# Differential attention: one projection of q and k for a head pair, with a weight ring of raw 2, hi 3, lo 3

## The chip, the core and the metric

The kernel runs on one core of a Trainium2 chip. The engines of that core are TensorE (PE in the profile, with its weight loads as PEld), VectorE (DVE), ScalarE (ACT) and GpSimd (POOL); SyncE (SP) issues most transfers. The metric is the device time of one execution in microseconds (us).

## The reference, cut to what matters

Two transformer blocks run over 512 tokens of 1024 features, in float32: a pooling mixer and a latent attention (MLA), each with a SwiGLU feed-forward stage, then a final norm, differential attention and a mixture of 16 experts. The change lies in the differential attention:

```python
def diff_attention(x, w_in, q_gain, k_gain, lq1, lk1, lq2, lk2, subln, w_out, lambda_init):
    H, dh = DA_HEADS, DA_HEAD_DIM
    q, k, v = jnp.split(x @ w_in, [2 * H * dh, 4 * H * dh], axis=-1)
    q = rmsnorm(q.reshape(B, T, H, 2, dh), q_gain) * (dh ** -0.5)
    k = rmsnorm(k.reshape(B, T, H, 2, dh), k_gain)
    v = v.reshape(B, T, H, 2 * dh)
    ...
    for s in range(0, T, QBLOCK):
        ...
        p = jax.nn.softmax(sc, axis=-1)
        pd = p[:, :, 0] - lam * p[:, :, 1]
        outs.append(jnp.einsum('bhqk,bkhe->bqhe', pd.astype(v.dtype), v[:, :e]))
    o = rmsnorm(jnp.concatenate(outs, axis=1), subln) * (1.0 - lambda_init)
    return o.reshape(B, T, H * 2 * dh) @ w_out
```

## The kernel before

**Products.** Each float32 factor is held as a high and a low part, so that one product is three matmuls (high by high, low by high, high by low), added up in an accumulator. Activations are kept transposed: `xh[k]`, `xl[k]` hold 128 features of all 512 tokens, for the eight slices k of the 1024 features. PSUM has eight banks of 512 float32 columns here: four of tag `acc`, two of tag `t` (transposes), two of tag `s` (scores).

**Weights.** `Stream` (`self.ws`) brings the weights as items of up to 2048 columns. `load` has SP transfer an item into a `raw` buffer; `split_part` makes a quarter's high part on ACT (`hi<-raw`) and its low part on DVE or POOL (`lo<-raw,hi`); `pump` does one such quarter if the rings `BUFS` (line 47) have room; `take` hands an item to its consumer and first splits what is missing; `release` gives `hi` and `lo` back. The expert weights use the same buffers later.

**Order.** All engines work in program order. The program's order is made when the kernel is built: generators are tasks of `Sched`, which runs the ready task of lowest rank by the times that `Plan` estimates for each engine. `get` takes a free PSUM bank, waiting in this planned time, and `put` gives it back. So a change in one place can move instructions of the rest of the stage on every engine.

**Differential attention.** `attention` runs two tasks. `feed` projects the four head pairs one after the other by `da_project(p, out)`; pair 0 and 1 at once, pair 2 and 3 when enough blocks of the earlier pairs are over (`LEAD`). `blocks` (higher priority) runs eight heads with four query blocks each: `da_scores` (tiles `pss`, `p`), `da_values` (`acc<-v,pth`, `on`, `o`). When all pairs are projected the heads' outputs are split (`oh`, `ol`) and the output products (`acc<-oh,hi` and so on) begin.

**A pair's projection.** In `da_project` the tokens are the stationary factor and the weights stream: for s = q, k, v and for each of four token tiles j, eight slices k with three matmuls of 256 columns, two tiles to an `acc` bank. Each of q, k and v is an item of 2048 columns. In pair 0 the first seven slices of two tiles of q come first (`early`), because the last slice `xh[7]` is the last that the feed-forward stage delivers. After the last slice of the first tile `da_norm` is started: it sums squares over the features (`pst<-ones,ss`), takes roots on POOL (`r1`, `r2`), and yields `r12` per token and R, r1 spread over all partitions by `pst<-ident,r`; then it updates `x` slice by slice on DVE. Each finished bank of q or k goes to `part(s, jj, ps)`: wait for `r12`, square on ACT (`sq<-acc`), sum by groups of 64 on DVE (`st<-sq`), scale (`st`, `rqkv`), power on POOL (`rqk<-rqkv,mhalf`), scale (`rqk`), and `qn<-acc,rqk` on DVE, which frees the bank. When both banks of q (or of k) are through, `turned(s)` transposes them head by head (`pst<-ident,qn`), and `q_parts` and `k_parts` split the result on ACT and DVE (`qh`, `ql`, `kh`, `kl`, `klh`, `kll`). `v_part` scales and splits v.

The lines that the steps touch are 47 (rings), 1340 to 1346 (`r12`), 1355 to 1489 (`da_project`), and the layout of `da_in` in `_host`.

## Time and profile before

| | us |
|---|---|
| three runs: median (lowest to highest) | 1568.91 (1567.87 to 1570.69) |
| the profiled execution | 1568.89 |
| its span on the core | 1567.1 |
| PE busy | 1495.6 (95%) |
| PE weight loads busy | 1233.7 (79%) |
| DVE busy | 1017.4 (65%) |
| ACT busy | 782.9 (50%) |
| POOL busy | 508.8 (32%) |

The stages by the order of time on PE: pooling to 36 us, feed-forward to about 430, MLA to 660 with its output products, feed-forward to 939, differential attention to about 1214 with its output products, routing to 1237, experts to the end. A busy share is an average over these stages. Matmuls are pipelined: a matmul's recorded duration overlaps the next one's, so the distance between two starts tells what one costs. In a row of the trace in order of time the brackets at the end give the idle time ahead of it on its engine and what ended that; the names are those of the program, output first.

### The profile page before, as it was taken

How to read it: one execution, taken by the hardware profiler on the slowest of the kernel's cores; microseconds unless marked ns; L12 is line 12 of the kernel's file. 1: busy time of each engine (PE TensorE's matmuls, PEld its weight loads, DVE VectorE, ACT ScalarE, POOL GpSimd, SP SyncE). 2: the span in 40 equal slices, each digit the busy share in tenths (PEclk: the TensorE clock that was granted, in tenths of full speed). 3: DMA queues.
4: the chain of work that ended last, by engine and by line, in shares of the span. 5: the costliest groups of instructions: out<-in, count | busy, mean ns of one | idle time of the engine just before them, and what ended most of it. 6: DMA issues, size and time to landing. Idle time of an engine off the chain costs nothing. (4 is left out here: it accounts for less than half of the span.)

```text
span 1567.1 us, 21562 instructions
## 1 busy us (share of the span) xinstructions
PE 1495.6 (95%) x7752; PEld 1233.7 (79%) x7752; DVE 1017.4 (65%) x1668; ACT 782.9 (50%) x1585; POOL 508.8 (32%) x382
## 2 busy tenths in 40 slices
PE   8999999999999999999999999999989699999996
PEld 7788888888878888888888889998978466666664
DVE  6564344445477754443444466988984699999996
ACT  5323222323366633332233345787783478787884
POOL 4322122311231113321232223322222466565553
PEclk9999999999999999999999999999989699999998
DMA  6121333223210223214322232211068889999961
GB/s 241 61 107 56 116 111 108 73 75 119 69 63 28 68 108 121 99 42 142 108 86 86 74 119 84 78 55 68 28 202 296 261 302 362 345 355 360 348 206 27
DMA packets 69935, 221.61 MB, mean 141 GB/s; under 512 B 7616, under 2 KB 16960, under 8 KB 56640
## 3 DMA queue, kind: packets, MB, share of 16 engines
q1 hardware_dynamic: 56448, 201.03, 35.9%
q0 software_dynamic: 4064, 14.16, 3.7%
q10 hardware_dynamic: 9312, 5.01, 1.1%
q8 instruction: 62, 1.02, 0.3%
q14 instruction: 49, 0.40, 0.1%
HBM read 208.63 MB, written 11.53 MB: 140 GB/s over the span
## 5 line engine op out<-in xcount | busy, mean ns | idle before, releaser
L341 POOL TENSOR_TENSOR lo<-raw,hi 128x512 fp32r<-128x512 f32 (+1 forms) x157 | 224.4, 1439 | 694.4 <-ACT hi L341 592.4
L341 PE MATMUL acc<-xh,hi 128*128 128x512 f32 x744 | 290.5, 390 | 0.3 <-ACT xh L341 0.3
L341 PE MATMUL acc<-xl,hi 128*128 128x512 f32 x744 | 289.6, 389 | 0.3 <-DVE xl L341 0.3
L341 PE MATMUL acc<-xh,lo 128*128 128x512 f32 x744 | 289.5, 389 | 0.0
L341 DVE TENSOR_TENSOR wl<-raw,wh 128x512 fp32r<-128x512 f32 x288 | 268.1, 982 | 6.1 <-ACT wh L341 5.7
L341 ACT ACTIVATE hi<-raw 128x512 fp32r<-128x512 f32 (+1 forms) x378 | 208.8, 607 | 86.1 <-issue 59.8
L341 DVE TENSOR_TENSOR lo<-raw,hi 128x512 fp32r<-128x512 f32 (+1 forms) x221 | 215.9, 987 | 19.6 <-ACT hi L341 18.9
L341 ACT ACTIVATE wh<-raw 128x512 fp32r<-128x512 f32 x384 | 211.8, 621 | 15.8 <-PE acc L341 10.0
L341 POOL TENSOR_TENSOR wl<-raw,wh 128x512 fp32r<-128x512 f32 x96 | 147.1, 1533 | 119.4 <-ACT wh L341 90.8
L341 PEld LDWEIGHTS acc<-xh,hi 128*128 128x128 f32 x744 | 139.7, 188 | 29.6 <-ACT xh L341 0.7
L341 PEld LDWEIGHTS acc<-xl,hi 128*128 128x128 f32 x744 | 139.7, 188 | 29.1 <-DVE xl L341 0.6
L341 PEld LDWEIGHTS acc<-xh,lo 128*128 128x128 f32 x744 | 139.6, 188 | 29.1
L341 DVE TENSOR_TENSOR u<-acc,R 128x512 f32<-128x512 f32 x44 | 30.4, 691 | 181.0 <-PE acc L341 181.0
L341 PE MATMUL acc<-hh,hi 128*128 128x512 f32 x352 | 136.9, 389 | 0.0
L341 PE MATMUL acc<-hl,hi 128*128 128x512 f32 x352 | 136.9, 389 | 0.0
L341 PE MATMUL acc<-hh,lo 128*128 128x512 f32 x352 | 136.9, 389 | 0.0
L341 ACT ACTIVATE hh<-t 128x512 fp32r<-128x512 f32 x44 | 27.8, 632 | 218.4 <-DVE t L341 218.4
L341 DVE TENSOR_TENSOR x<-acc,x 128x512 f32<-128x512 f32 x59 | 40.5, 690 | 121.0 <-PE acc L341 120.9
L341 PE MATMUL acc<-hi,xh 128*128 128x256 f32 x384 | 111.0, 289 | 0.0
L341 PE MATMUL acc<-lo,xh 128*128 128x256 f32 x384 | 108.7, 283 | 0.6 <-DVE lo L341 0.6
L341 PE MATMUL acc<-hi,xl 128*128 128x256 f32 x384 | 108.5, 283 | 0.0
L341 PE MATMUL acc<-wl,teh 128*96 128x512 f32 x256 | 102.5, 401 | 3.3 <-POOL wl L341 1.7
(314 smaller groups left out, 2917.9 us busy)
## 6 DMA issues: line engine op xcount, KB each, us to landing
raw<-moe_w SPq DMA_DIRECT2D x200, 256.0 KB, 7.1
raw<-moe_w SPq DMA_DIRECT2D x46, 1024.0 KB, 7.3
raw<-ffn_gu SPq DMA_DIRECT2D x43, 1024.0 KB, 4.8
raw<-ffn_dn SPq DMA_DIRECT2D x32, 704.0 KB, 4.0
raw<-da_in SPq DMA_DIRECT2D x12, 1024.0 KB, 4.7
raw<-mla_up SPq DMA_DIRECT2D x4, 832.0 KB, 4.4
raw<-mla_o_a SPq DMA_DIRECT2D x12, 256.0 KB, 4.3
raw<-da_o_a SPq DMA_DIRECT2D x12, 256.0 KB, 3.9
```

Of the source, the lines that this page charges most:

```text
L341: r = f(*args, **kw)
```

## The change

- q and k of a pair are projected together. `da_in` is laid out anew on the host: a pair's first two items hold q's and k's 256 columns side by side, slices 0 to 3 in the first and 4 to 7 in the second; the third item is v's, as before. For each token tile the eight slices now take three matmuls of 512 columns each, which fill one `acc` bank. Two items are held during this phase. v keeps its 256 columns and two tiles to a bank.
- In pair 0 the first seven slices of all four tiles come first, then the last slices.
- `part(j, ps)` handles one tile with q and k side by side. Its scaling uses `r12qk`, a small table that `da_norm` fills with two more copies.
- `turned` for q and for k start when all four tiles are through; v's projection follows the tiles at once.
- `pump` is called twice per tile in both phases.
- The rings are raw 2, hi 3, lo 3 instead of raw 3, hi 3, lo 2, for the whole kernel.

```diff
--- before.py
+++ after.py
@@ -44,7 +44,7 @@
 GATHER = 7.0
 CAP = 96
 SLACK = -1.0
-BUFS = {"raw": 3, "hi": 3, "lo": 2}
+BUFS = {"raw": 2, "hi": 3, "lo": 3}
 EPS = 1e-6
 WINDOWS = (2, 4, 8, 16)
 LAMBDA_INIT = 0.8 - 0.6
@@ -1344,6 +1344,10 @@
         self.r12q = c.tile([P, NT], F32, name="r12q")
         nc.vector.tensor_scalar(self.r12q, r12, 0.125, None, op0=OP.mult)
         self.r12 = r12
+        self.r12qk = c.tile([P, NT, 8], F32, name="r12qk")
+        for i, r in enumerate((self.r12q, r12)):
+            nc.vector.tensor_copy(self.r12qk[:, :, 4 * i:4 * i + 4],
+                                  r[:, :, None].to_broadcast([P, NT, 4]))
         R = self.bcast(r1, "R1", ps[0])
         self.put("t", 2)
         for d in range(KT):
@@ -1356,7 +1360,8 @@
         nc, sched = self.nc, self.sched
         qn = {}
 
-        def part(s, jj, ps):
+        def part(j, ps):
+
             yield from self.wait("r12")
             q = self.tmp("sq")
             nc.scalar.activation(q, ps, AF.Square)
@@ -1364,31 +1369,27 @@
             st = self.small.tile([P, 8], F32, name="st", tag="st", bufs=6)
             nc.vector.tensor_reduce(st, q.rearrange("p (a b) -> p a b", b=64), axis=AX.X,
                                     op=OP.add)
-            sh = [P, 2, 4]
-            v = st.rearrange("p (a b) -> p a b", b=4)
-            j = slice(2 * jj, 2 * jj + 2)
-            nc.vector.tensor_tensor(v, v, self.r12s[:, j][:, :, None].to_broadcast(sh), op=OP.mult)
+            nc.vector.tensor_scalar(st, st, self.r12s[:, j:j + 1], None, op0=OP.mult)
             r = self.rstd(st, 64, "rqk")
             yield r
-            f = r.rearrange("p (a b) -> p a b", b=4)
-            rr = (self.r12q if s == 0 else self.r12)[:, j]
-            nc.vector.tensor_tensor(f, f, rr[:, :, None].to_broadcast(sh), op=OP.mult)
+            nc.vector.tensor_tensor(r, r, self.r12qk[:, j], op=OP.mult)
             t = self.tmp("qn")
             nc.vector.tensor_tensor(t.rearrange("p (a b) -> p a b", b=64),
                                     ps.rearrange("p (a b) -> p a b", b=64),
                                     r[:, :, None].to_broadcast([P, 8, 64]), op=OP.mult)
             self.put("acc")
             yield t
-            qn[s, jj] = t
-            if (s, 1 - jj) in qn:
-                sched.spawn(turned(s), 1)
+            qn[j] = t
+            if len(qn) == NT:
+                for s in range(2):
+                    sched.spawn(turned(s), 1)
 
         def turned(s):
             for hd in range(2):
                 pt = yield from self.get("t")
                 for j in range(NT):
-                    c = (j % 2) * 256 + hd * P
-                    self.turn(pt[:, j * P:(j + 1) * P], qn[s, j // 2][:, c:c + P])
+                    c = s * 256 + hd * P
+                    self.turn(pt[:, j * P:(j + 1) * P], qn[j][:, c:c + P])
                 yield pt
                 out["qk"[s] + str(hd)] = yield from (q_parts(pt) if s == 0 else k_parts(pt))
 
@@ -1452,41 +1453,48 @@
 
         xh, xl = self.xh, self.xl
 
-        def product(w, ps, j, ks):
-            o = ps[:, (j % 2) * 256:(j % 2 + 1) * 256]
+        def product(ws, o, j, ks, n):
             t = slice(j * P, (j + 1) * P)
+            per = KT // len(ws)
             for k in ks:
-                c = slice(k * 256, (k + 1) * 256)
+                w, c = ws[k // per], slice(k % per * n, (k % per + 1) * n)
                 self.mm(o, xh[k][:, t], w[0][:, c], start=(k == 0), stop=False)
                 self.mm(o, xl[k][:, t], w[0][:, c], start=False, stop=False)
                 self.mm(o, xh[k][:, t], w[1][:, c], start=False, stop=(k == KT - 1))
-                if k == 3:
+                if k % 4 == 3:
                     self.ws.pump()
-                if k % 4 == 3 and k < KT - 1:
+                    if k < KT - 1:
+                        yield 0.0
+
+        w = [self.ws.take(), self.ws.take()]
+        ps = [None] * NT
+        if p == 0:
+
+            for j in range(NT):
+                ps[j] = yield from self.get("acc")
+                yield from product(w, ps[j], j, range(KT - 1), T)
+        for j in range(NT):
+            if ps[j] is None:
+                ps[j] = yield from self.get("acc")
+            yield from product(w, ps[j], j, range(KT - 1 if p == 0 else 0, KT), T)
+            if p == 0 and j == 0:
+                sched.spawn(self.da_norm(), 0)
+            if j == NT - 1:
+                for x in w:
+                    self.ws.release(x)
+            sched.spawn(part(j, ps[j]), 1, ps[j])
+            yield 0.0
+        w = [self.ws.take()]
+        for jj in range(2):
+            ps = yield from self.get("acc")
+            for j in range(2):
+                yield from product(w, ps[:, j * 256:(j + 1) * 256], 2 * jj + j, range(KT), 256)
+                if j == 0:
                     yield 0.0
-
-        for s in range(3):
-            w = self.ws.take()
-            ps = [None, None]
-            early = (p, s) == (0, 0)
-            if early:
-
-                for jj in range(2):
-                    ps[jj] = yield from self.get("acc")
-                    yield from product(w, ps[jj], 2 * jj, range(KT - 1))
-            for j in range(NT):
-                if ps[j // 2] is None:
-                    ps[j // 2] = yield from self.get("acc")
-                begun = early and j % 2 == 0
-                yield from product(w, ps[j // 2], j, range(KT - 1 if begun else 0, KT))
-                if early and j == 0:
-                    sched.spawn(self.da_norm(), 0)
-                if j == NT - 1:
-                    self.ws.release()
-                if j % 2:
-                    i = j // 2
-                    sched.spawn(part(s, i, ps[i]) if s < 2 else v_part(i, ps[i]), 1, ps[i])
-                yield 0.0
+            if jj == 1:
+                self.ws.release(w[0])
+            sched.spawn(v_part(jj, ps), 1, ps)
+            yield 0.0
 
     def da_scores(self, d, hd, qb, h, done):
         nc = self.nc
@@ -2118,8 +2126,10 @@
         w = w[0].reshape(KT, P, 4, 2, P)
         o[name + "_a"] = f(w[:6].transpose(2, 1, 3, 0, 4).reshape(4, P, 1536))
         o[name + "_b"] = f(w[6:].transpose(1, 2, 3, 0, 4).reshape(P, 2048))
-    o["da_in"] = f(inp["da_w_in_2"][0].reshape(KT, P, 3, 4, 256).transpose(3, 2, 1, 0, 4)
-                   .reshape(4, 3, P, 2048))
+    w = inp["da_w_in_2"][0].reshape(KT, P, 3, 4, 256)
+    qk = w[:, :, :2].reshape(2, 4, P, 2, 4, 256).transpose(4, 0, 2, 1, 3, 5).reshape(4, 2, P, 2048)
+    v = w[:, :, 2].transpose(2, 1, 0, 3).reshape(4, 1, P, 2048)
+    o["da_in"] = f(np.concatenate([qk, v], axis=1))
     we = np.concatenate([inp["moe_w_group_2"][0], inp["moe_w_router_2"][0]], axis=1)
     o["router"] = f(we.reshape(KT, P, 20).transpose(1, 0, 2))
     o["router_b"] = f(np.concatenate([inp["moe_b_group_2"][0], inp["moe_b_router_2"][0]]))
```

**Where instructions move.** PE, first head pair: three last rows of the projection before the transposes `pst<-ident,r` of `da_norm`, and what stands behind them (`acc<-hi,xh` is a projection matmul, xh stationary and hi the weights; waits in brackets are for an engine's earlier instructions). Before:

```order
L341 MATMUL acc<-hi,xh 128x256
L341 MATMUL acc<-hi,xl 128x256
L341 MATMUL acc<-lo,xh 128x256
L341 MATMUL pst<-ident,r_7119 128x128 [waits Pool_49]
L341 MATMUL pst<-ident,r_7119 128x128 x3
L341 MATMUL acc<-hi,xh 128x256
L341 MATMUL acc<-hi,xl 128x256
L341 MATMUL acc<-lo,xh 128x256
```

Now:

```order
L341 MATMUL acc<-hi,xh 128x512
L341 MATMUL acc<-hi,xl 128x512
L341 MATMUL acc<-lo,xh 128x512
L341 MATMUL pst<-ident,r_7176 128x128 [waits Pool_49]
L341 MATMUL pst<-ident,r_7176 128x128 x3
L341 MATMUL acc<-hi,xh 128x256 [waits DVE_49,Activation_49]
L341 MATMUL acc<-hi,xl 128x256
L341 MATMUL acc<-lo,xh 128x256
```

The transposes stood in the middle of q's second tile, with q and k to go; they now stand between the last matmuls of q and k and the first of v, which takes a bank that DVE and ACT have to free.

DVE, first head pair: from a reduction of a part's squares (`st<-sq`) to the first `qn` (`lo` is a weight's low part, `x` the update by `da_norm`). Before, from the first part's reduction:

```order
L341 TENSOR_REDUCE st<-sq 128x8 [waits Activation_49]
L341 TENSOR_TENSOR st<-st,r12s 128x8 [waits DVE_49]
L341 TENSOR_SCALAR rqkv<-st 128x8 [waits DVE_49]
L341 TENSOR_TENSOR lo<-raw,hi 128x512 [waits Activation_49]
L341 SCALAR_TENSOR_TENSOR x<-x,vecs,R_7164 128x512
L341 TENSOR_REDUCE st<-sq 128x8 [waits Activation_49]
L341 TENSOR_TENSOR st<-st,r12s 128x8 [waits DVE_49]
L341 TENSOR_SCALAR rqkv<-st 128x8 [waits DVE_49]
L341 TENSOR_TENSOR rqk<-rqk,r12q 128x8 [waits Pool_49]
L341 TENSOR_TENSOR qn<-acc,rqk 128x512 [waits DVE_49,PE_49]
```

Now, from the third part's reduction (the first and second part's three rows each stand right ahead):

```order
L341 TENSOR_REDUCE st<-sq 128x8 [waits Activation_49]
L341 TENSOR_SCALAR st<-st,r12s 128x8 [waits DVE_49]
L341 TENSOR_SCALAR rqkv<-st 128x8 [waits DVE_49]
L341 TENSOR_REDUCE st<-sq 128x8 [waits Activation_49]
L341 TENSOR_SCALAR st<-st,r12s 128x8 [waits DVE_49]
L341 TENSOR_SCALAR rqkv<-st 128x8 [waits DVE_49]
L341 SCALAR_TENSOR_TENSOR x<-x,vecs,R_7211 128x512
L341 TENSOR_TENSOR rqk<-rqk,r12qk 128x8 [waits Pool_49]
L341 TENSOR_TENSOR qn<-acc,rqk 128x512 [waits DVE_49]
```

The first `qn` stood behind the reductions of two parts; it now stands behind those of four.

ACT, last head pair: around the last two instructions of `v_part` (`v<-acc`). Before:

```order
L341 ACTIVATE kh<-kh 64x512 [waits Activation_49]
L341 ACTIVATE kl<-kl 64x512 [waits Activation_49]
L341 ACTIVATE v<-acc,r_7154 128x2x128 [waits PE_49]
L341 ACTIVATE v<-acc,r_7154 128x2x128
L341 ACTIVATE klh<-klh 64x512 [waits DVE_49]
L341 ACTIVATE kll<-kll 64x512 [waits DVE_49]
L341 ACTIVATE pth<-pst 128x512 [waits PE_49]
```

Now:

```order
L341 ACTIVATE v<-acc,r_7198 128x2x128 [waits PE_49]
L341 ACTIVATE v<-acc,r_7198 128x2x128
L341 ACTIVATE qh<-pst,vecs 64x512 [waits PE_49]
L341 ACTIVATE ql<-pst,vecs 64x512
L341 ACTIVATE kh<-pst,vecs 64x512 [waits PE_49]
L341 ACTIVATE kl<-pst,vecs 64x512
L341 ACTIVATE kh<-kh 64x512 [waits Activation_49]
L341 ACTIVATE kl<-kl 64x512 [waits Activation_49]
L341 ACTIVATE o<-pst,sub 128x256 [waits PE_49]
L341 ACTIVATE klh<-klh 64x512 [waits DVE_49,Pool_49]
L341 ACTIVATE kll<-kll 64x512 [waits DVE_49]
```

k of that pair's first head was split ahead of the last v, but for the two copies `klh` and `kll`; now it is split behind it, and q of the second head (`qh`, `ql`) stands in between.

## Rows read from the trace of the kernel before

**Rows 1.** The page, part 1: busy time, share of the span and instructions.

```profile
PE 1495.6 (95%) x7752; PEld 1233.7 (79%) x7752; DVE 1017.4 (65%) x1668; ACT 782.9 (50%) x1585; POOL 508.8 (32%) x382
```

**Rows 2.** Busy time by stage (stretch, length, engines, PEclk, DMA share, GB/s).

```profile
440.00:660.00 220.00, 216.35 (x1146) 182.01 (x1145) 140.48 (x259) 110.66 (x242) 54.71 (x53) 1.00 0.21 72
1000.00:1120.00 120.00, 116.85 (x955) 115.08 (x954) 106.90 (x292) 90.04 (x230) 35.07 (x28) 1.00 0.15 54
```

**Rows 3.** Groups by line and form, PE, 930 to 1140 us (count | busy us, mean ns | idle before).

```profile
L341 PE MATMUL acc<-lo,xh 128*128 128x256 f32 x384 | 108.7, 283 | 0.6 <-DVE lo L341 0.6
```

**Rows 4.** PE in time, last matmuls of the feed-forward stage (start, duration, us).

```profile
935.64 0.39 PE L341 MATMUL acc<-hh,lo 128*128 128x512 f32 x1
...
939.27 0.28 PE L341 MATMUL acc<-hi,xh 128*128 128x256 f32 x1
```

**Rows 5.** PE in time, first pair: row sums, transposes, projection.

```profile
944.66 1.84 PE L341 MATMUL pst<-ones,ss 128*128 128x1 f32 x16
946.37 0.36 PE L341 MATMUL acc<-hi,xh 128*128 128x256 f32 x1
...
949.32 1.05 PE L341 MATMUL pst<-ident,r 128*128 128x128 f32 x8
...
950.45 0.28 PE L341 MATMUL acc<-lo,xh 128*128 128x256 f32 x1
...
959.08 0.28 PE L341 MATMUL acc<-lo,xh 128*128 128x256 f32 x1
```

**Rows 6.** DVE in time, first pair: reductions, scale, qn, x.

```profile
951.53 0.69 DVE L341 TENSOR_REDUCE st<-sq 128x8 f32<-128x512 f32 x1 [1.78 <-ACT sq L341]
...
952.53 0.68 DVE L341 TENSOR_TENSOR lo<-raw,hi 128x512 fp32r<-128x512 f32 x1
...
955.28 0.16 DVE L341 TENSOR_TENSOR rqk<-rqk,r12q 128x8 f32<-128x8 f32 x1
955.54 0.69 DVE L341 TENSOR_TENSOR qn<-acc,rqk 128x512 f32<-128x512 f32 x1
...
959.01 0.74 DVE L341 SCALAR_TENSOR_TENSOR x<-x,vecs,R 128x512 f32<-128x512 f32 x1
```

**Rows 7.** ACT in time, first pair: R and first square.

```profile
950.41 0.60 ACT L341 ACTIVATE R<-pst 128x512 f32<-128x512 f32 x1 [6.79 <-PE pst L341]
950.90 0.59 ACT L341 ACTIVATE sq<-acc 128x512 f32<-128x512 f32 x1
```

**Rows 8.** POOL in time, first pair: first power.

```profile
945.89 1.03 POOL L341 TENSOR_TENSOR r<-r1v,mhalf 128x4 f32<-128x4 f32 x1 [1.23 <-DVE r1v L341]
```

**Rows 9.** PE in time, the attention's end.

```profile
1127.74 0.60 PE L341 MATMUL pst<-ident,p 128*128 128x128 f32 x4
...
1130.99 0.34 PE L341 MATMUL pss<-kll,ql 128*128 128x128 f32 x1 [0.21 <-ACT kll L341]
...
1133.54 0.41 PE L341 MATMUL acc<-v,pth 128*128 128x256 f32 x1
...
1136.31 0.41 PE L341 MATMUL acc<-v,ptl 128*128 128x256 f32 x1
```

**Rows 10.** Busy time by stretch at the attention's end.

```profile
1131.00:1138.00 7.00, 6.13 (x27) 5.98 (x28) 3.71 (x15) 3.89 (x13) 0.00 (x0) 0.51 0.00 0
1138.00:1144.80 6.80, 3.19 (x15) 1.80 (x14) 6.31 (x20) 6.58 (x18) 0.70 (x1) 1.00 0.32 86
```

**Rows 11.** The transfers of da_in.

```profile
DMA to landing us min/median/max: 4.7/4.7/5.5
```

**Rows 12.** PE in time, first output product.

```profile
1151.25 0.78 PE L341 MATMUL acc<-oh,hi 128*128 128x512 f32 x1
```

**Rows 13.** ACT in time, last head pair's splits.

```profile
1124.93 0.67 ACT L341 ACTIVATE kh<-pst,vecs 64x512 fp32r<-64x512 f32 x1
...
1127.50 0.63 ACT L341 ACTIVATE kh<-kh 64x512 fp32r<-64x512 f32 x1
...
1128.79 0.84 ACT L341 ACTIVATE v<-acc,r 128x256 fp32r<-128x256 f32 x2
```


## The prediction

> **What bounds the kernel now.** I read the page first: TensorE (PE) is busy 95% of the span, the next engine, VectorE (DVE), 65% [rows 1]. Then the busy time by stage: from 1000 to 1120 us, where differential attention projects q, k and v of the later head pairs between the score blocks of the earlier ones, PE is idle for 3.2 us of 120 at its upper clock (1.00, which is 2.4 GHz), and DVE is busy 89% [rows 2]. So a microsecond less on PE there is nearly a microsecond less of the whole, a pause of PE is lost, and DVE is close behind. After 1120 us no projection is left to fill the waits of the attention, and the clock falls to its lower level (0.51, 1.2 GHz) for a stretch [rows 10]. Last come the views in order of time of PE, DVE, ScalarE (ACT) and GpSimd (POOL) around the first pair's projection, since the change rewrites it.
>
> **The change, part by part.**
>
> *Fewer, longer matmuls.* The projections are 1152 matmuls of 256 columns, in three groups of 384 of which one is shown [rows 3]; 768 of them are q and k and become 384 of 512 columns. Recorded durations overlap, so the price is the distance between starts. In the 512-column stream of the stage before it is (939.27 - 935.64) / 16 = 0.2269 us [rows 4]; in the 256-column stream it is (959.08 - 950.45) / 72 = 0.1199 us [rows 5]. Hence 768 x 0.1199 = 92.1 us become 384 x 0.2269 = 87.1 us: **-5.0 us**, 1.25 in each pair. Bounds: -5.0, and 0 if a long one costs as much here as two short ones.
>
> The Trainium skill, "TensorE: Matmul & The Clock Gate", section "Back-to-back issue gap", gives columns / 2.4 + 2.5 ns for a lone gap at the full clock. By that page this would be, as an estimate, 2.5 ns for each two, 1.0 us in all, and the sum below would end 4 us higher; the rows show 13 ns for each two, and the rows decide.
>
> *The accumulators of the first pair.* This step decides, I think. There are four accumulator banks ("acc"). Before, the first pair's q takes two, its k the other two, and v gets the first one back only after k. After, each of the four token tiles of q and k takes a bank, all four are opened with seven of eight slices before any last slice, and v follows at once. A bank comes back when `part` has written its `qn`; `part` first needs the norms of `da_norm`, and that starts when the first tile's last slice is done. The two PE pieces in the section on the change show it: before, short matmuls without a wait stand behind the transposes `ident,r`; after, v's first matmul stands there and waits for DVE and ACT.
>
> Count from the start of the sums `ones,ss`. PE has 1.71 us of sums (944.66 to 946.37), then only nine matmuls (9 x 0.2269 = 2.04 us) and 1.05 us of `ident,r`: it runs dry at +4.8 us [rows 5]. The chain that frees the first bank: POOL's first power is done at 946.92, +2.26 [rows 8], so `ident,r` starts when PE reaches it, +3.75; its copy R on ACT begins 1.09 us later (949.32 to 950.41), +4.84; the first square 0.49 us after that, +5.33 [rows 5, 7]; the first reduction 0.63 us later, +5.96 [rows 6]. From here the order on DVE tells: all four parts' reductions stand ahead of the first `qn`, each 1.00 us with its two small steps (951.53 to 952.53), so +9.96; then the 0.74 us update of x, 0.26 us for the scale (955.28 to 955.54) and 0.69 us for `qn`: +11.65 us [rows 6]. POOL's power for eight columns, about twice the 1.03 us for four [rows 8], hides behind the reductions. Before, the chain took 944.66 to 956.23, 11.6 us as well, covered by 99 projection matmuls. PE now stands still for 11.65 - 4.8: **+6.9 us**. Bounds: 6 and 8, since the nearest rows leave only single steps of up to 1.0 us (a reduction, a split between) in doubt.
>
> The Trainium skill, "Perfetto Trace Analysis", section "Matmuls", says that independent matmul groups should rotate through the PSUM banks, so that one's evacuation overlaps the next group's matmuls, and that larger matmuls are more efficient. The two pull apart here: in this pair the rows give the second 1.25 us and the first 6.9 us.
>
> *The clock after that pause.* Near 1131 us the pauses of the attention's end (one of 0.21 us is shown, its neighbours are 0.5 to 0.9) go over into 7 us at the lower level [rows 9, 10], where short matmuls start every (1136.31 - 1133.54) / 13 = 0.213 us [rows 9] instead of 0.120. A pause of 7 us should bring such a stretch. What falls into the pause costs nothing; if half of it, 3.5 us, falls on v's matmuls, 44% of that is lost: **+1.5 us**, bounds 0 (no fall) and 3.1 (all 7 us on work).
>
> *Pairs 1 to 3.* Here the banks' evacuation is covered by score blocks. But q and k now end together, their transposes and splits bunch, and DVE, at 89%, keeps its work while PE's shrinks by 3.75 us: I take a quarter of that as eaten by new waits, **+1.0 us**, bounds 0 and 3.75.
>
> *The ring.* A 1 MB transfer lands in 4.7 us, 5.5 at most [rows 11], and a gate-and-up tile feeds 48 long matmuls, 48 x 0.2269 = 10.9 us, so two raw buffers hide the load. q and k are held together while v is split, and each phase of a pair has eight chances to split, as many as q and k have quarters. The one wait for a split weight in the projections, 0.6 us [rows 3], may go. Zero; bounds -0.6 and, if the cover is gone once, +1. PE's order also differs in the last third of the earlier (MLA) attention, whose stage idles 3.65 of 220 us [rows 2]: zero, bounds -1.5 and +1.5. The scaling on DVE keeps its count, 16 parts of 128x512: zero.
>
> *The end of the attention.* From the last projection (1127.74) to the first output product (1151.25) it takes 23.5 us [rows 9, 12]. Afterwards, by the ACT pieces in the section on the change, ACT splits the first head's k, and the second head's q ahead of that, behind the last v instead of ahead of it: two v (0.84 together), four splits (0.67 each), four copies (0.63 each) [rows 13], 6.0 us until the first score block can end, where before it ended 3.6 us after the last projection (1130.99 + 0.34 [rows 9]). Against these 2.4 us, 20 value matmuls and 14 transposes have left this stretch, some 3 us. I take zero; -10 and +5 belong to the rivals.
>
> *Sum.* The profiled execution took 1568.89 us (span 1567.1); the median of the three runs is 1568.91, the same. -5.0 + 6.9 + 1.5 + 1.0 = +4.4: **1573.3 us**.
>
> **The rivals.**
>
> *The end of the attention shrinks (the other side).* Place: between the last projection and the first output product. In 1138 to 1144.8 us PE was busy 3.19 of 6.8 us [rows 10]. If the work that has left takes such a gap with it, 6.8 us go, and with fewer pauses the clock stays up for the rest, some 3 us more: -10, 1563.3 us. It decides once more than 4.4 us are won there. For it: fewer items, output products one score block earlier. Against: the longer queue on ACT.
>
> *The pause is milder.* The clock stays up and no new waits come: -5.0 + 6.9 = +1.9, 1570.8 us. For it: when v runs, ACT and DVE have just emptied their queues. Against: the shorter pauses near 1131 us already went with the lower clock.
>
> *The bunched splits delay the later pairs.* If the first score block of the last pair starts 2.4 us late as above, with nothing gained behind it, and the two pairs before lose half of that each, +5 in all: 1578.3 us. For it: DVE at 89%.
>
> *The long matmuls do not save here*, so that the change does not do what it says: +5.0, 1578.3 us too. Against: the stage right before shows 0.2269 us.
>
> **How the numbers follow.** Forecast 1573.3, own range 1571.3 to 1575.5: 0.40. Milder pause 1570.8: 0.25. Bunched splits 1578.3: 0.20. No saving: 0.05. Shorter end 1563.3: 0.10. A measurement of this kernel can tell about 0.2%, 3.1 us, from no change, so 1565.8 to 1572.0 counts as the same. Slower: 0.31 of the forecast's 0.40 and the two high cases, 0.56. The same: 0.09 of the forecast, the milder pause and a tenth of the shorter end, 0.35. Faster: 0.09. The range leaves out most of the shorter end below and the upper third of the two high cases: 1566.0 to 1580.0.
>
> **What would show it.** In the profile after: one pause of PE of 6 to 8 us ahead of v's first matmul, ended by DVE's `qn`; a lower granted clock right behind it; 384 matmuls of 512 columns in the projections, 0.227 us apart; the chain from `ones,ss` to the first `qn` again 11.6 us long. The forecast is wrong if that pause is under 4 us, if the stretch from the last projection to the first output product changes by more than 5 us, or if PE waits for split weights or raw transfers in any stage.

## The result

In four executions each, the changed kernel took 1592.5 us (median; 1589.6 to 1600.6) and the kernel before 1569.8 us (1567.9 to 1571.7). The ratio is **1.0153 (95% interval 1.0112 to 1.0194)**: slower, as forecast, but by 22.7 us where 4.4 were forecast, and above the upper end of the range (1580). The profiled execution of the changed kernel took 1594.4 us with a span of 1592.6, 25.5 more than the 1567.1 of before.

Part 1 of its page, to be held against [rows 1], shows 384 matmuls less and PE busy *longer*:

```profile
PE 1501.8 (94%) x7368; PEld 1220.7 (77%) x7368; DVE 1016.3 (64%) x1669; ACT 782.7 (49%) x1585; POOL 516.2 (32%) x383
```

A lower clock makes each matmul take longer, so busy time alone does not tell where the 25.5 us went. The places where PE starts something new do. The table gives the starts of five PE rows in each trace (first projection matmul, first matmul of the second pair, last projection matmul, first and last output product) and the distances between them.

| us | before | after | difference | forecast |
|---|---|---|---|---|
| start of the first projection | 939.3 | 945.6 | +6.4 | 0 |
| first pair | 38.5 | 46.9 | +8.4 | +7.15 (6.9 + 1.5 - 1.25) |
| pairs 1 to 3, to the last projection matmul | 149.8 | 160.0 | +10.2 | -2.75 (1.0 - 3.75) |
| from there to the first output product | 23.6 | 20.1 | -3.5 | 0 |
| output products, first to last | 62.5 | 65.7 | +3.2 | 0 |
| from the last output product to the end of the span | 353.4 | 354.2 | +0.8 | 0 |
| sum | 1567.1 | 1592.6 | +25.5 | +4.4 |

So the first pair went as forecast, and two stages that I had put at zero and below cost 16.6 us. The busy time by stage of the changed kernel (columns as in [rows 2], whose two stretches come first; then pairs 1 to 3 and the output products, and below them the same two stages of the kernel before):

```profile
440.00:660.00 220.00, 214.07 (x1118) 179.31 (x1118) 140.69 (x254) 107.15 (x235) 54.18 (x50) 0.98 0.19 63
1000.00:1120.00 120.00, 109.30 (x656) 97.42 (x655) 101.01 (x284) 89.57 (x226) 28.32 (x23) 0.94 0.17 60
...
992.56:1152.55 159.99, 149.29 (x915) 133.81 (x914) 132.97 (x368) 114.62 (x291) 41.69 (x33) 0.96 0.18 62
...
1172.69:1238.35 65.66, 63.99 (x342) 54.07 (x343) 39.90 (x90) 30.28 (x78) 15.16 (x14) 0.97 0.72 247
```

```profile
977.78:1127.62 149.84, 145.78 (x1189) 143.18 (x1187) 132.93 (x364) 115.13 (x290) 41.37 (x32) 1.00 0.17 61
1151.25:1213.69 62.44, 62.14 (x333) 53.19 (x332) 40.46 (x79) 30.00 (x73) 18.09 (x16) 0.97 0.87 295
```

In 1000 to 1120 us PE was idle for 3.2 us before and is for 10.7 now, and DVE is *less* busy (101.0 against 106.9): PE does not wait because DVE has more to do, but for single results.

**The first pair.** PE in order of time (start, duration; in brackets the idle time ahead and what ended it; rows left out are marked by three dots):

```profile
945.63 0.39 PE L341 MATMUL acc<-hi,xh 128*128 128x512 f32 x1
...
965.36 1.84 PE L341 MATMUL pst<-ones,ss 128*128 128x1 f32 x16
...
969.24 1.05 PE L341 MATMUL pst<-ident,r 128*128 128x128 f32 x8
977.40 0.55 PE L341 MATMUL acc<-hi,xh 128*128 128x256 f32 x1 [7.11 <-DVE rqk L341]
...
984.06 1.04 PE L341 MATMUL pst<-ident,qn 128*128 128x128 f32 x8
```

From the first row of the 512-column stream to the sums there are 87 matmuls: (965.36 - 945.63) / 87 = 0.2268 us each, as [rows 4] had it. Then the pause of 7.11 us ahead of v, with the reason that was forecast. Behind it the granted clock is 0.50 (1.2 GHz) in this row:

```profile
972.30:982.50 10.20, 5.10 (x24) 5.13 (x25) 9.82 (x23) 2.12 (x5) 8.56 (x5) 0.50 0.07 28
```

and v's first 36 matmuls take 984.06 - 977.40 = 6.66 us, 2.3 more than 36 x 0.1199. DVE shows the chain that PE waited for; from the start of the sums to the end of the first `qn` it is 977.25 - 965.36 = 11.9 us:

```profile
971.45 0.69 DVE L341 TENSOR_REDUCE st<-sq 128x8 f32<-128x512 f32 x1 [0.95 <-ACT sq L341]
...
974.63 0.68 DVE L341 TENSOR_REDUCE st<-sq 128x8 f32<-128x512 f32 x1
...
975.70 0.74 DVE L341 SCALAR_TENSOR_TENSOR x<-x,vecs,R 128x512 f32<-128x512 f32 x1
...
976.56 0.69 DVE L341 TENSOR_TENSOR qn<-acc,rqk 128x512 f32<-128x512 f32 x1
```

**The ends of the later pairs.** The waits of PE from 930 to 1260 us (us in total, times, longest):

```profile
PE pst L341 <- DVE ql L341: 9.1, 4, 4.0
PE acc L341 <- DVE rqk L341: 7.1, 1, 7.1
...
PE pst L341 <- DVE kll L341: 4.1, 2, 3.6
```

Beside the 7.1 us of the first pair, those for `ql` and `kll` are new in this size: 13.2 us together, 9.9 of them in pairs 1 to 3, where the kernel before has 0.4 us for `ql` and none for `kll` (0.5 right behind the last projection). At the end of pair 1 it looks like this, PE first, then ACT and DVE in the same stretch:

```profile
1034.88 1.03 PE L341 MATMUL pst<-ident,qn 128*128 128x128 f32 x8
...
1038.59 0.63 PE L341 MATMUL pst<-ident,qn 128*128 128x128 f32 x4 [1.25 <-DVE ql L341]
1042.81 0.66 PE L341 MATMUL pst<-ident,on 128*128 128x128 f32 x2 [3.60 <-DVE kll L341]
1043.12 0.78 PE L341 MATMUL acc<-hi,xh 128*128 128x512 f32 x1
1043.69 0.63 PE L341 MATMUL acc<-hi,xl 128*128 128x512 f32 x1
```

```profile
1035.52 0.68 ACT L341 ACTIVATE qh<-pst,vecs 64x512 fp32r<-64x512 f32 x1 [2.41 <-PE pst L341]
...
1036.92 0.72 ACT L341 ACTIVATE p<-p,nm 128x512 f32<-128x512 f32 x1
...
1038.35 0.61 ACT L341 ACTIVATE hi<-raw 128x512 fp32r<-128x512 f32 x1
...
1039.71 0.68 ACT L341 ACTIVATE kh<-pst,vecs 64x512 fp32r<-64x512 f32 x1
1040.42 0.68 ACT L341 ACTIVATE kl<-pst,vecs 64x512 fp32r<-64x512 f32 x1
```

```profile
1037.68 0.76 DVE L341 SCALAR_TENSOR_TENSOR ql<-pst,vecs,ql 64x512 fp32r<-64x512 f32 x1
...
1041.91 0.76 DVE L341 SCALAR_TENSOR_TENSOR kll<-pst,vecs,kl 64x512 fp32r<-64x512 f32 x1
```

The eight transposes at 1034.88 fill both banks of tag `t`. A bank comes back when ACT has made `qh` and `ql` and DVE has subtracted (1038.44), and the next only after `kh`, `kl` on ACT, which stand behind two softmax rows, a weight split and two squares, and `klh`, `kll` on DVE (1042.67). PE has twelve short matmuls of v left and then stands for 1.25 and 3.60 us; the first matmul of pair 2, at 1043.12, is queued behind. The next matmuls are 0.43 us apart instead of 0.227: the clock is at its lower level from 1040.6 to 1047.4. Pairs 2 and 3 end in the same way, with 4.01 and 3.26 us as the longest wait for `ql`.

### The profile page after: what moved, and what is told of

The parts are those of the page before. It is cut to its first block, busy times and chain, and to the rows that moved or that the text cites. A ratio compares the mean times of both kernels' runs of the same rounds, so it can differ in the third digit from the quotient of the medians.

```text
span 1592.6 us, 20794 instructions
## 1 busy us (share of the span) xinstructions
PE 1501.8 (94%) x7368; PEld 1220.7 (77%) x7368; DVE 1016.3 (64%) x1669; ACT 782.7 (49%) x1585; POOL 516.2 (32%) x383
## 5 line engine op out<-in xcount | busy, mean ns | idle before, releaser
L341 POOL TENSOR_TENSOR lo<-raw,hi 128x512 fp32r<-128x512 f32 (+1 forms) x158 | 231.2, 1474 | 728.9 <-ACT hi L341 627.4
L341 ACT ACTIVATE wh<-raw 128x512 fp32r<-128x512 f32 x384 | 212.0, 621 | 17.8 <-PE acc L341 10.7
L341 PE MATMUL acc<-wh,teh 128*96 128x512 f32 x256 | 105.7, 413 | 0.0
L341 PE MATMUL acc<-wh,tel 128*96 128x512 f32 x256 | 102.7, 401 | 0.0
L341 PE MATMUL acc<-hi,xh 128*128 128x512 f32 (+1 forms) x256 | 89.9, 351 | 7.1 <-DVE rqk L341 7.1
```

What stands on the lines that cost most here:

```text
L341: r = f(*args, **kw)
```

## The experiments

In all of them stage lengths are the distances of the table above. The arena of 57 tiles leaves no room for some orders with 28 expert pieces loaded ahead at routing, so some runs have 27 (`AHEAD`), and two controls tell what that costs.

**The rings alone.** The kernel before with 27 pieces and

```diff
-BUFS = {"raw": 3, "hi": 3, "lo": 2}
+BUFS = {"raw": 2, "hi": 3, "lo": 3}
```

> The kernel before with the rings of the changed kernel alone (raw 2, hi 3, lo 3); the number of expert pieces loaded ahead at routing is 27 instead of 28, here and in the runs beside it, since the arena of 57 tiles is full otherwise. Theory: the 6.4 us by which differential attention starts later in the changed kernel's trace (945.63 against 939.27) come from the rings, so its first projection starts at 945 to 946 us here too, with the waits for xh at the start of the second feed-forward stage and a stretch at the lower clock behind them, and the whole takes 1575 to 1577 us. Rival (my forecast's zero for the rings): the start stays at 939 to 940 and the whole at 1567 to 1571 us.

Measured: 1591.2 us, ratio 1.0158 (1.0139 to 1.0177), as much as the whole change. The first projection starts at 944.7, so the 6.4 us ahead of it come with the rings. ACT at the start of the second feed-forward stage, of this run, shows why:

```profile
586.46 0.63 ACT L341 ACTIVATE hi<-raw 128x512 fp32r<-128x512 f32 x1 [8.10 <-DMA raw<-ffn_gu]
587.00 0.70 ACT L341 ACTIVATE xh<-x,vecs 128x512 fp32r<-128x512 f32 x1
```

ACT stands 8.10 us at the first split of a gate-and-up tile, whose transfer has not landed; `xh` is queued behind it, and PE's matmuls wait for that `xh`. In all eight traces with these rings this wait is 8.1 to 8.3 us; in the nine with the old rings there is none. The windows 560 to 580 and 580 to 600 us of the changed kernel, then of before, tell the same of the transfers (the last three columns are PEclk, DMA share, GB/s):

```profile
560.00:580.00 20.00, 20.00 (x90) 16.57 (x89) 10.49 (x17) 6.12 (x10) 0.00 (x0) 1.00 0.00 0
580.00:600.00 20.00, 18.43 (x75) 14.72 (x74) 5.39 (x8) 6.18 (x10) 3.99 (x3) 0.83 0.44 158
```

```profile
560.00:580.00 20.00, 20.00 (x90) 16.57 (x89) 10.85 (x17) 8.52 (x15) 1.30 (x1) 1.00 0.29 109
580.00:600.00 20.00, 20.00 (x98) 16.79 (x97) 9.95 (x14) 6.28 (x10) 6.04 (x9) 1.00 0.36 126
```

With three raw buffers the next tile is brought in during 560 to 580 us; with two nothing moves there, SP issues it 13 us later, and PE loses 1.6 us at the start of the stage, 2.3 in the row 440 to 660 against [rows 2], and in some traces 7 us at the lower clock behind it. SP's issues, changed kernel, then before:

```profile
579.41 12.79 SPq L124 DMA_DIRECT2D raw<-ffn_gu  x3
```

```profile
566.19 33.80 SPq L124 DMA_DIRECT2D raw<-ffn_gu  x5
```

The first projection starts at 942.8 to 946.2 us in the seven traces with the new rings and the builder's estimate of a matmul unchanged, and at 939.3 to 941.4 in the four with the old rings. That accounts for 1.4 to 6.9 of the 25.5 us. (The start alone would not show it: with the old rings and a changed estimate, below, it lies anywhere from 939.2 to 947.3 us. The wait of ACT does.) But this kernel loses another 15.6 us between the first projection (944.7) and the last output product (1234.7; 290.0 us instead of 274.4), without any edit of the projection. The theory did not have that. The builder splits weights elsewhere with these rings, and PE's order differs from that of the kernel before from 500 us on. PE waits for no split weight in this attention, so I put the 15.6 us down to the new order; no run separates the two.

**Control: 27 pieces.**

```diff
-AHEAD = (24, 28, 32)
+AHEAD = (24, 27, 32)
```

The kernel before with it:

> The kernel before with 27 instead of 28 expert pieces loaded ahead at routing, as in the four runs before this one. It tells what that setting alone costs. If nothing (1567 to 1571 us, output products from first to last 62 to 63 us), the 23 us of the run with the rings alone are the rings'. If it costs, the output products take 78 to 81 us here too and the experts some 4 us more: 1585 to 1591 us; the rings then have at most the 5.5 us ahead of the first projection and what the pairs show.

The changed kernel with it:

> The changed kernel with 27 instead of 28 expert pieces ahead. If the setting costs nothing: 1590 to 1596 us as the changed kernel. If it costs 16 to 21 us as the difference between the output products of the runs before suggests: 1606 to 1614 us, and the two runs with a mended order (1585 and 1587 us) then gained 20 us and more, not 5 to 7.

Measured: 1574.0 us, ratio 1.0039 (1.0025 to 1.0053), and 1591.9 us, 1.0155 (1.0135 to 1.0175). Up to the last output product the setting changes nothing: 38.5, 149.8, 23.6 and 62.5 us in the first, 46.4, 161.0, 20.1 and 64.8 us in the second. The first run's order of instructions on PE, DVE, ACT and POOL differs from that of the kernel before only from 1521 us on, in the experts, and its cost is 0.4%; the traced execution (1569.3 us, the fastest of ten) does not show where. Since the second executes the same PE order as the changed kernel, it also tells how well a stage repeats: within 1.1 us.

**Is it the order?** Four runs of the kernel before in which only the builder's estimate of a matmul's time is changed by 0.2 to 0.9%; the instructions are the same, their order changes, and each new order is called a draw (it differs for three of them from 448 us on, within the MLA attention, for 2350 from 972 us on).

```diff
-            price = 0.109 if name == "transpose" else max(n, 256) / 2370 if t == F32R \
+            price = 0.109 if name == "transpose" else max(n, 256) / 2360 if t == F32R \
```

> The kernel before, with the builder's estimate of a matmul raised by 0.4% (2360 instead of 2370 columns per us) and nothing else: the same instructions, in another order from the second pair on. It measures what a mere change of the drawn order costs. Theory: the order before is a good draw, and another one loses 5 to 20 us between the first projection and the first expert, with the same kinds of waits (transposes, scores, ol). Rival: orders are alike, 1567 to 1572 us; what the rings alone cost (17 us more than the run with 27 pieces) is then the rings' own mechanism.

> The same with the estimate lowered by 0.4% (2380 columns per us): a second draw of the order of the kernel before. Theory: 1573 to 1590 us; rival: 1567 to 1572 us.

> The kernel before with the builder's estimate of a matmul lowered by 0.2% (2375 columns per us): a third draw of its order. Draw theory: 1577 to 1592 us, as the two draws before (1580.5, 1587.8). Rival: the order before is an ordinary one and those two were bad: 1567 to 1572 us.

> The kernel before with that estimate raised by 0.9% (2350 columns per us): a fourth draw. Draw theory: 1577 to 1592 us; rival: 1567 to 1572 us.

| | median, us | ratio (95%) | start | first projection to last output product |
|---|---|---|---|---|
| before, beside them | 1566.6, 1567.8 | 1 | 939.3 | 274.4 |
| 2375 | 1575.1 | 1.0046 (1.0033 to 1.0060) | 943.2 | 278.8 |
| 2380 | 1580.5 | 1.0083 (1.0065 to 1.0100) | 947.3 | 283.6 |
| 2350 | 1585.2 | 1.0108 (1.0083 to 1.0133) | 939.2 | 281.9 |
| 2360 | 1587.8 | 1.0135 (1.0118 to 1.0152) | 941.6 | 283.8 |

All four are slower than before; 2375 fell below its expectation by 2 us. In the attention a new order costs 4.4 to 9.4 us; 2350 and 2360 lose some 7 us more in the experts (from the last output product to the end 360 to 361 us against 353.4), 2375 and 2380 gain 2.8 there. Pairs 1 to 3 alone take 152.2, 153.2, 155.6 and 162.5 us (2375, 2350, 2360, 2380) against 149.8, with the short matmuls of before. The waits are small ones at many places; PE in pairs 1 to 3 of the run with 2360:

```profile
PE acc L341 <- DVE lo L341: 1.4, 1, 1.4
PE pss L341 <- ACT klh L341: 1.4, 1, 1.4
PE pst L341 <- DVE kll L341: 1.3, 1, 1.3
PE pss L341 <- DVE nm L341: 1.0, 1, 1.0
```

So the order before is better than five others that were tried with the same work (these four and the one that the rings draw), and each new draw here gave some of that up. The same for the changed kernel, with the estimate at 2380:

> The changed kernel with the builder's estimate lowered by 0.4% (2380 columns per us): a second draw of its order. The pause of 7 us in the first pair is in the code's order (four banks), not in the draw, and should stand in every draw; the standing at the transposes behind v of pairs 1 to 3 should stand too if it comes from q and k ending together. Theory: 1585 to 1605 us with both still there. Rival: the draw is all, and another one may come out at 1575 us or less.

Measured: 1590.5 us, ratio 1.0155 (1.0138 to 1.0172); the attention takes 290.8 us, against 292.7. The pause ahead of v is there again with 7.1 us, and `ql` and `kll` with 3.0 and 3.6 us. The pause stands in every kernel that opens four tiles (7.3 us with the rings of before, below), the standing at the transposes in both draws of the changed kernel, but not in every draw of its projection, as the next run shows.

**The pause of the first pair, taken away.** Only two tiles are opened ahead of the last slices (27 pieces):

```diff
-            for j in range(NT):
+            for j in range(2):
                 ps[j] = yield from self.get("acc")
...
-            yield from product(w, ps[j], j, range(KT - 1 if p == 0 else 0, KT), T)
+            yield from product(w, ps[j], j, range(KT - 1 if p == 0 and j < 2 else 0, KT), T)
```

> The changed kernel, but in the first pair only two token tiles are opened with seven slices ahead of the last ones, so da_norm starts 9.5 us of matmuls earlier against the end of q and k. Theory: the two whole tiles left, 48 matmuls of 0.227 us, cover the chain of 11.6 us, the pause before v's first matmul goes, and the low clock behind it; the first pair takes 37 to 39 us instead of 46.9 and the whole 1582 to 1585 us. Rival: the banks are the limit whatever the order, and the pause only moves (to the last tiles or into v): 1588 us or more.

Measured: 1585.4 us, ratio 1.0130 (1.0099 to 1.0162). The first pair takes 37.35 us, without a pause and at the upper clock:

```profile
942.81:980.16 37.35, 37.35 (x229) 33.52 (x228) 22.56 (x49) 15.21 (x27) 13.30 (x9) 1.00 0.24 85
```

That is 9.6 us less than in the changed kernel and 1.15 less than in the kernel before, nearly the 1.25 that the long matmuls were to save there. The theory holds for its place. The last projection matmul comes at 1129.0 instead of 1152.5, but the output products take 78.7 us instead of 65.7, and of 23.5 us gained 9.6 are left at the last output product.

Pairs 1 to 3 of this run, and all of PE's waits there above 1 us:

```profile
980.16:1129.02 148.86, 143.99 (x884) 128.88 (x883) 129.31 (x360) 113.48 (x284) 39.55 (x31) 0.98 0.18 66
```

```profile
PE pst L341 <- ACT o L341: 2.5, 2, 2.3
PE pst L341 <- DVE on L341: 1.4, 1, 1.4
```

q and k of a pair end together here too, but PE waits for neither `ql` nor `kll`, and the stage is 1.0 us shorter than before. The loss of this run lies in the output products instead, 78.7 us against 62.4. So the form of the projection alone does not bring the standing; the order must also leave PE nothing else to do.

**The standing at the transposes, taken away.** The feed may project pairs 2 and 3 eight blocks ahead (27 pieces):

```diff
-LEAD = ((6, 6), (4, 2))
+LEAD = ((6, 6), (8, 8))
```

> The changed kernel with the third and fourth pair's projection allowed eight blocks ahead (4 and 2 before), so that projection matmuls stand between the transposes of q and k of pairs 1 and 2. Theory: PE stands at these transposes since four groups come at once, two banks take them and nothing else is queued; with projection work in between the standing goes (pairs 1 and 2: 5.4 and 7.0 us, and the low clock behind it), while the attention's end gets longer by up to 6 us as less work is left there to interleave: 1580 to 1587 us. Rival: ACT and DVE cannot keep up in these stages, the same waits come at other places: 1590 us or more.

Measured: 1587.3 us, ratio 1.0118 (1.0101 to 1.0135). Pairs 1 to 3 take 136.7 us instead of 160.0, at the full clock, and PE's waits from 930 to 1130 us are these:

```profile
PE acc L341 <- DVE rqk L341: 7.1, 1, 7.1
PE acc L341 <- DVE lo L341: 0.5, 1, 0.5
PE acc L341 <- DVE ptl L341: 0.2, 1, 0.2
```

So the standing was for want of other work, as the theory had it. Then the gain is given back: the two rows are pairs 1 to 3 and the output products.

```profile
993.07:1129.73 136.66, 135.86 (x848) 121.57 (x847) 120.10 (x329) 106.74 (x262) 39.13 (x31) 1.00 0.20 72
1147.40:1232.37 84.97, 77.31 (x411) 65.62 (x409) 51.45 (x128) 41.77 (x116) 17.07 (x17) 0.92 0.54 182
```

22.8 us ahead of the changed kernel at the last projection matmul, it is 6.0 us ahead at the last output product. 68 value and 28 score matmuls stand among the output products now, where the changed kernel has 40 and 12, and PE waits for their results (the longest wait there is 4.3 us, for `ptl`); DVE is busy for only 51.5 of the 85.0 us. The projection was the filling of the attention; what is filled early is missing late.

Both repairs (27 pieces), with the lead eight blocks for pair 2 and four for pair 3:

```diff
-LEAD = ((6, 6), (4, 2))
+LEAD = ((6, 6), (8, 4))
```

> The changed kernel (its rings, 27 pieces ahead) with both repairs: two tiles opened ahead in the first pair (gained about 10 us up to the first expert) and the third pair's projection allowed eight blocks ahead instead of four. If the two gains add: first pair 37 to 38 us, no standing at the transposes at the end of pair 1, 1575 to 1582 us. If what is won by filling one place is lost at the next, since DVE and ACT are 85 to 95% busy there: 1584 us or more, as with each repair alone (1585, 1587).

Measured: 1589.2 us, ratio 1.0131 (1.0105 to 1.0156); first pair 37.3, pairs 1 to 3 150.2, output products 78.2 us. The gains do not add; `ql` and `kll` still cost 2.7 and 2.1 us.

**A bank counted as free later.** After q's and k's splits the builder adds 3 us to the time at which a transpose bank is free (the same line in both places; 27 pieces):

```diff
             self.put("t")
+            self.free["t"][-1] += 3.0
```

> The changed kernel (27 pieces) in which the builder counts a transpose bank as free 3 us later after q's and k's splits, so that other ready work is put ahead of the next transposes. Theory: PE's standing at the ends of pairs 1 to 3 is an order made with too short a time for the splits, and shrinks from 4 us to 1 to 2 us a place; by its stages up to the last projection it gains 5 to 9 us on the run with 27 pieces and nothing else changed. Rival: nothing else is ready there, PE waits as long under another name; the last projection ends at 1150 to 1155 us as before.

Measured: 1616.0 us, ratio 1.0307 (1.0290 to 1.0325), the slowest of all. `ql` shrinks to 2.7 us, but the scores now wait for the later `kh` and `klh`, 4.7 and 4.1 us; the last projection matmul starts at 1150.9, and the output products take 82.0 us. The rival was right: it is not a wrong estimate at one place.

**The rings of before.** The changed kernel with raw 3, hi 3, lo 2 (27 pieces):

> The changed kernel with the rings of before (raw 3, hi 3, lo 2): the projection part of the change alone. Theory: the first projection starts at 939 to 940 us, the rest is as in the changed kernel (7 us pause in the first pair, 4 to 5 us of standing at the transposes of each later pair), 1585 to 1588 us. Rival: with two lo buffers, both held while q and k are projected, v's split comes late; PE then waits for a split weight at each v, 1 to 3 us a pair, and the whole is 1590 us or more.

Measured: 1601.0 us, ratio 1.0209 (1.0192 to 1.0226). It starts early, at 941.4, and then the rival comes: both lo buffers are held through q and k, and v waits for its split. PE's waits from 930 to 1150 us:

```profile
PE acc L341 <- DVE rqk L341: 7.3, 1, 7.3
PE acc L341 <- ACT hi L341: 4.0, 4, 2.0
PE acc L341 <- DVE lo L341: 3.0, 3, 2.0
```

The same rings with two tiles opened ahead (28 pieces), and a second draw of that with the estimate at 2360:

> The changed kernel with both repairs that need no new order by hand: two instead of four tiles opened ahead in the first pair, and the rings of before (28 pieces ahead, as in the two kernels). Theory: no pause before v in the first pair, the start of the projection back at 939 to 941 us, and the long matmuls' 5 us saved; PE still stands at the transposes at the ends of the pairs: first pair 37 to 38 us, whole 1566 to 1574 us. Rival (the time follows the order the builder happens to draw, not these parts): anywhere up to 1590 us with the loss behind the last projection.

> The changed kernel with two tiles opened ahead in the first pair and the rings of before (1586.4 us as drawn first), with the builder's estimate raised by 0.4% (2360 columns per us): a second draw of the repaired kernel. If the long matmuls' 5 us are kept behind the draw: 1575 to 1586 us, mean of the repaired kernels 4 to 6 us below the draws of before. If the form of the projection eats them in pairs 1 to 3: 1583 to 1592 us.

Measured: 1586.4 us, ratio 1.0121 (1.0104 to 1.0138), and 1596.3 us, 1.0173 (1.0148 to 1.0198); from first projection to last output product 291.2 and 291.8 us (the second loses 7.7 us more in the experts, much as 2360 did with the kernel before). The theory of the first (1566 to 1574) failed, and the second lies above both of its ranges. The first pair takes 40.0 us, and v's weights cost 4.8 and 4.9 us. So the new projection needs the third lo buffer, and raw 2 is what the feed-forward stage pays for it.

## Why the prediction failed, point by point

| first projection to last output product | us |
|---|---|
| before | 274.4 |
| before, five new orders (2375, 2350, 2380, 2360, rings) | 278.8, 281.9, 283.6, 283.8, 290.0 |
| changed, repaired (two tiles; lead; both; two tiles with the rings of before, twice) | 286.0, 286.2, 287.3, 291.2, 291.8 |
| changed (2380; with 27 pieces; as it is) | 290.8, 292.4, 292.7 |
| changed, rings of before; bank counted later | 303.8, 311.3 |

*Fewer, longer matmuls, -5.0: right as a price of PE's work.* 0.2268 us each in the changed kernel; in the run without the pause the first pair shows 1.15 of its 1.25 us. In the whole no run shows the 5 us.

*The accumulators of the first pair, +6.9: right.* 7.11 us, and with two tiles opened ahead it is gone. The chain was 11.9 us instead of 11.65. (Two readings are off without bearing on the sum: 75 projection matmuls, not 99, cover the chain of before, and the row at 1127.74 is a transpose, behind the last projection matmul at 1127.62.)

The Trainium skill, "Perfetto Trace Analysis", section "Matmuls", asks that independent matmul groups rotate through the banks; the trace agrees, since with all four banks held until the norms were there the next group stood for 7.11 us.

*The clock behind it, +1.5: right in kind.* The lower level holds from 972.3 to 982.5; 2.3 us of it fall on v.

*Pairs 1 to 3, new waits +1.0 (0 to 3.75): the step that failed.* They cost 10.2 + 3.75 = 14 us: PE's idle time there rose from 4.1 to 10.7 us, and in two stretches at the lower level PE was busy for 10.2 us, of which half, 5 us, is lost, as an estimate; the remaining 2 us I cannot place. I saw that "their transposes and splits bunch" and priced it as a quarter of a saving on DVE. In this kernel the price lay in the order: q's and k's four transpose groups need two banks, each bank is held through an ACT and a DVE queue, and behind v nothing is left to fill until the feed is let on. The rows were there: a group takes two ACT splits of 0.67 us [rows 13], so four take 4 x 1.34 = 5.4 us on ACT alone, of which twelve matmuls of v (12 x 0.12 = 1.4 us) hide a part. That is 4 us a pair, as an estimate, and the lower clock with it, as near 1131 us [rows 10]. The run with the longer lead shows that the standing goes when other work is queued. But the form alone does not bring it: with two tiles opened it did not come, and pairs 1 to 3 took 1.0 us less than before. And a new order alone, with the old form, made this stage 2.3 to 12.7 us longer (the four changed estimates). So how much of the 14 us is the form and how much the draw stays open.

*The ring, 0 (-0.6 to +1): failed too, at another place than I looked, and costs 1.4 to 6.9 us.* I held a transfer (4.7 us) against the 10.9 us in which one gate-and-up tile feeds PE, which is right within the stage. The cost came at the border of two stages, where the next tile's transfer could not be issued until a raw buffer was free, and ACT's queue held `xh` behind it, so that PE came to wait on a raw transfer, which the prediction had named as a sign of being wrong. The bound should have come from a look at when SP issues the first tile of a stage.

*The order in the rest, 0 (MLA -1.5 to +1.5): failed as a premise.* Each term was a difference to the order of before, with everything else as it stands there. The runs with a changed estimate show that, against the four other orders drawn, this order is worth 4.4 to 9.4 us in the attention alone and 7 to 21 us in the whole. The widest bound that I gave for a moved order was 1.5 us.

*The end of the attention, 0:* -3.5 and then +3.2 in the output products: 0 in sum, though not for the reason that I gave, as the run with the longer lead shows.

*Rivals.* "The bunched splits delay the later pairs" (1578.3) had the right place for this draw, and a third of the size. That the kernel gets slower was forecast for a reason that explains the 8.4 us of the first pair out of 25.5; for the rest the right direction was luck. "The end of the attention shrinks" was -3.5 there and was given back at once. The pause was not milder, and the long matmuls did save.

What stays open is the share of the new form of the projection beside that of the draw. The five repaired kernels of the table take 286 to 292 us, the five new orders of the kernel before 279 to 290: the 5 us of the long matmuls do not show, and the loss lies in other stages from draw to draw (pairs 1 to 3 as it is, the output products with two tiles or the longer lead). The ranges overlap, and no changed kernel was drawn as well as the kernel before. No version here beats the kernel before.

## What to carry to other kernels

Where a builder draws the order of a tuned kernel from estimates, price a new order as a cost of its own, and measure it by one neutral change of an estimate; here it was larger than every term that could be read from the diff. When two results of one stage are made to end together, count the banks that take them and the queues through which a bank comes back, and look for the work that PE has meanwhile. When a repair wins time in one stage, look for it at the end of the next one: here half of it and more was gone there. Size a ring at the borders of stages too, where the first transfer of the next stage has to be issued.

## What the runs showed of the hardware

A pause of 3 to 4 us at the end of each later pair went over into 6.8 us and more at the lower level of the clock. The changed kernel, pairs 1, 2 and 3 (PEclk is the third number from the end):

```profile
1040.60:1047.40 6.80, 4.59 (x12) 3.75 (x13) 4.90 (x8) 6.08 (x11) 0.40 (x1) 0.50 0.07 10
1098.60:1105.40 6.80, 5.57 (x24) 5.04 (x25) 5.25 (x19) 4.92 (x14) 0.70 (x1) 0.50 0.01 2
1156.70:1177.20 20.50, 13.70 (x40) 10.24 (x41) 16.75 (x49) 20.10 (x45) 0.46 (x1) 0.50 0.50 157
```

After the last of them there is no projection left, and the level stays down for 20.5 us. And in the run with the longer lead, whose pairs 1 to 3 have no wait above 0.5 us, the clock there was 1.00. PE is busy for 23.9 us in these three rows; at the lower level half of that, some 12 us, is lost, as an estimate, which is about as much as the 13.2 us of waits for `ql` and `kll`. The prediction had counted such a loss only for the first pair.
